# Decoder layer on one core: q and k transposed by DMA in 16-bit halves, probabilities joined by VectorE, other banks for two gates

## The chip, the cores and the metric

The kernel runs on 1 core of one Trainium2 chip. The metric is the device time of one execution in microseconds (us). Engines: TensorE (PE for matmuls, PEld for its weight loads), VectorE (DVE), ScalarE (ACT), GpSimd (POOL) and SyncE (SP, which issues the DMAs). L387 is line 387 of the kernel.

## What is computed

One decoder layer for 256 positions of width 1024, in float32:

```python
proj  = x @ W_in                      -> [q | k | v | B | C | h | gate_attn | gate_conv]
y_att = MoBA block-sparse causal attention(q, k, v) @ W_att   (partial rotary on q, k)
y_cnv = (B * causal_dwconv3(C * h)) @ W_cnv
mix   = (sigmoid(g_att) * y_att + sigmoid(g_cnv) * y_cnv) @ W_o
x     = LayerNorm(alpha * x + mix)
u     = causal_dwconv3(x @ W_up);  f = (silu(u_gate) * u_val) @ W_down
x     = LayerNorm(alpha * x + f)
```

There are 8 heads of 64; the rotary turns the first 16 columns of each head. With 256 positions there is one block, so the attention is a plain causal softmax over it.

## The kernel before

**Two words for one.** Every product is made from a high and a low part. ScalarE rounds a float32 weight unit to the matmul's type (`split_h`, L203, "wh"), VectorE subtracts that from the original (`split_l`, L213, "wl"), and TensorE adds up high x high, high x low and low x high. Activations are split in the same way.

**Units and slots.** The weights come in chunks of 1 MB over SP's DMA queue into three buffers (`issue_dma`, L179). A chunk holds two units of 128x1024. After q, k and v (8 chunks, lines 614 to 670) come 28 units: h, c and b of the first half of the convolution, h, c, b of the second, then 16 gates. C0 is the first of them. `slot(u)` writes the program around unit u: its products on TensorE, then the list "pe" and the list "act" of that slot, then `split_h` up to unit u+5, then the list "first", then `split_l` up to u+4, then the list "dve". Nothing is reordered later: each engine runs its own instructions in the order in which they are written, and waits for what they need. `at(C0 + n, part, f)` puts a step at the end of a list, `at_once` at its head.

**A pair of units** (`two_units`, `cols_pair`): the first unit's wide products (L342) fill its PSUM bank, then the second's, then the narrow products (L349) end both. Two units on, ScalarE copies half of the bank out and VectorE adds the other half (`conv_sum_act` and `conv_sum_dve`, L677 and L681; `gate_sum_act` and `gate_sum_dve`, L729 and L733); then the bank is free. `gate` (L736) is the sigmoid.

**PSUM.** There are two pools of four banks each. Their banks are handed out in turn, and the first product in a bank waits until the last reader of the tile that had it before is done. The pool `acc` holds the banks of q and k, then those of the units. The pool `ps` holds the warm-up, v, the transposes of q and k, the scores, the products with v (`attend`) and the gates 0, 1, 6 and 7.

**The attention**, in steps that stand at fixed slots:

- `evac_rows` (L548): ScalarE copies q and k out of PSUM; `rope` (L376 to L379) turns 16 columns of each head in place, on VectorE, in slots 0 and 1.
- `qk_transpose` (L387, slot 2): TensorE turns 16 blocks of 128x128. `qk_h` (L394) and `qk_l` (through L232), slot 3: ScalarE and VectorE split them from PSUM into `qkT`.
- `scores` (L415): q times k for two head pairs, in slots 4 and 9.
- For each of the four head pairs p: `masks_low` (L422, ScalarE, then GpSimd), `masked` (L432, VectorE), `exps` (L444, ScalarE; the first needs a table load), `normalize` (L454, VectorE).
- The probabilities are transposed by DMA, which turns 16-bit elements: `probs_halves` (L462, VectorE) parts the words into a block of low and a block of high halves, `probs_T` (L466) turns 12 blocks of 128x128 over SP's queue, `probs_words` (L470, ScalarE) joins them again.
- `probs_h` (L473) and `probs_l` (L232) split them, `attend` (L485) multiplies by v, `attend_out` (L494, ScalarE and GpSimd), `attend_sum` (L502, VectorE), `attend_h` (L505) and `attend_l` make the input `aT` of the output product.

**The convolution** (`conv1` to `conv4`, L686 to L707) runs beside it. Behind the 28 units come the output products y (two PSUM banks for each of 8 column blocks), the product with W_o, the first norm, and the feed-forward part.

The lists of slots for the four head pairs, before:

```python
    for p, (m, e, n, tr, w, h, l, av) in enumerate(((5, 6, 8, 9, 12, 12, 13, 14), (7, 8, 11, 13, 15, 16, 16, 18),
                                                    (10, 11, 14, 16, 18, 18, 19, 22), (12, 13, 17, 19, 21, 22, 22, 24))):
```

m is masked, e exps, n normalize and probs_halves, tr probs_T, w probs_words, h and l the split, av attend.

## Time and profile before

| | |
|---|---|
| median of 3 runs | 361.46 us (361.29 to 361.51) |
| the profiled execution | 361.25 us |
| its span in the profile | 359.5 us |
| granted TensorE clock | 0.995 |

How to read it: the page gives the busy time of each engine and its share of the span; PE counts matmuls, whose ends are modelled, so PE can look busy while it only goes from one to the next. A waits line is "engine line <- what ended the wait: us in total, times, longest". The chain is what ended last, in order of time: start, length, engine, tile and line. A group line is "line engine operation out<-in shapes xcount | busy us, mean ns of one | idle before". A windows line is the stretch, its length, and the busy time and count of PE, PEld, DVE, ACT and POOL, then the granted clock, the DMA share and GB/s. A timeline line is start, length, engine, line, operation; merged instructions have a count. All times are from the start of the span.

### The profile page before, as it was taken

Reading aid. Unit: us, or ns where it says so; the run is one execution under the profiler, and the core shown is the slowest. Engines: PE = TensorE matmul, PEld = TensorE weight load, DVE = VectorE, ACT = ScalarE, POOL = GpSimd, SP = SyncE. Lnnn points to the kernel's source line nnn. Section 1 sums busy time; section 2 is a strip of 40 time slices with the busy share of each in tenths; the row PEclk is TensorE's granted clock in tenths of the full one; section 3 lists DMA queues with packets and bytes.
Section 4 is the critical chain, followed back from the end, with each engine's and each line's share of the span. In section 5 each row is a group of like instructions: output and inputs, shape, how many; then the busy total and the mean of one; then the engine's idle time right before and its main releaser. Section 6 shows DMA issues by size and latency. Waiting matters only on the chain.

```text
span 359.5 us, 5201 instructions
## 1 busy us (share of the span) xinstructions
PE 352.1 (98%) x1915; PEld 304.3 (85%) x1915; DVE 302.2 (84%) x522; ACT 238.9 (66%) x415; POOL 22.1 (6%) x49
## 2 busy tenths in 40 slices
PE   9999999999999999999999999999999999999993
PEld 8888889888887888888888888888888888988883
DVE  4687987999888989989769789997869696999875
ACT  4586768699999976652557466766647475677800
POOL 2000001100000112310000000000000000000110
PEclk9999999999999999999999999999999999999998
DMA  8979663753955765679061736538091735663002
GB/s 284 323 263 338 221 240 122 246 168 129 261 170 174 301 228 190 216 297 339 15 233 74 277 129 224 202 148 343 19 338 59 295 127 225 233 232 120 1 33 85
DMA packets 17370, 71.20 MB, mean 198 GB/s; under 512 B 7488, under 2 KB 8000, under 8 KB 10304
## 3 DMA queue, kind: packets, MB, share of 16 engines
q1 hardware_dynamic: 16768, 68.77, 53.2%
q0 software_dynamic: 576, 2.10, 2.0%
q8 instruction: 15, 0.25, 0.3%
q14 instruction: 11, 0.09, 0.1%
HBM read 68.24 MB, written 1.05 MB: 193 GB/s over the span
## 4 chain that ended last, share of the span: by engine, by line
PE 78%; ACT 10%; DVE 7%; issue 3%; POOLq 0%; POOL 0%; DVEq 0%; ACTq 0%
PE pb L342 20%; PE pb L349 11%; PE d L324 5%; PE d L325 5%; PE d L326 4%; PE y L342 4%; PE k L614 3%; PE v L614 3%; ACT wh L203 3%; PE q L614 3%; DVE wl L213 2%; PE y L349 2%; PE o L324 2%; PE o L326 2%; PE o L325 2%
## 5 line engine op out<-in xcount | busy, mean ns | idle before, releaser
L213 DVE TENSOR_TENSOR wl<-raw,wh 128x1024 fp32r<-128x1024 f32 x99 | 121.4, 1230 | 25.3 <-ACT wh L203 25.1
L203 ACT ACTIVATE wh<-raw 128x1024 fp32r<-128x1024 f32 x99 | 103.8, 1055 | 30.5 <-DMA raw<-in_wpack 30.3
L342 PE MATMUL pb<-x1T,wh 128*128 128x512 f32 x320 | 76.2, 390 | 0.0
L342 PEld LDWEIGHTS pb<-x1T,wh 128*128 128x128 f32 x320 | 59.7, 188 | 12.1
L349 PEld LDWEIGHTS pb<-x1T,wl 128*128 128x128 f32 x320 | 41.0, 191 | 1.6
L349 PE MATMUL pb<-x1T,wl 128*128 128x256 f32 x320 | 41.5, 283 | 0.0
L342 PE MATMUL g<-xT,wh 128*128 128x512 f32 x128 | 31.6, 393 | 0.6 <-DVE gs L733 0.6
L236 DVE TENSOR_TENSOR wl<-raw,wh 128x1024 fp32r<-128x1024 f32 (+2 forms) x29 | 27.0, 974 | 5.0 <-ACT wh L235 4.8
L235 ACT ACTIVATE wh<-raw 128x1024 fp32r<-128x1024 f32 (+2 forms) x29 | 23.4, 853 | 9.8 <-DMA raw<-in_wpack 5.8
L324 PE MATMUL d<-wh,f 128*128 128x512 f32 x76 | 29.8, 392 | 0.0
L325 PE MATMUL d<-wl,f 128*128 128x512 f32 x76 | 29.8, 391 | 0.0
L326 PE MATMUL d<-wh,f 128*128 128x512 f32 x76 | 29.6, 389 | 0.0
L342 PEld LDWEIGHTS g<-xT,wh 128*128 128x128 f32 x128 | 23.2, 188 | 5.5 <-PE av L486 0.8
L902 ACT ACTIVATE fb<-pb 128x512 f32<-128x512 f32 x20 | 11.9, 595 | 13.1 <-PE pb L349 13.1
L920 DVE SCALAR_TENSOR_TENSOR fc<-fb,consts,fc 128x254 f32<-128x254 f32 x40 | 19.3, 483 | 1.4
L918 DVE SCALAR_TENSOR_TENSOR fc<-fb,consts,fc 128x255 f32<-128x255 f32 x40 | 19.2, 480 | 0.0
L912 ACT ACTIVATE fc<-fb,consts 128x256 f32<-128x256 f32 x40 | 18.0, 499 | 0.6 <-DVE fb L906 0.6
L349 PEld LDWEIGHTS g<-xT,wl 128*128 128x128 f32 x128 | 16.4, 191 | 0.7
L326 PEld LDWEIGHTS d<-wh,f 128*128 128x128 f32 x76 | 14.3, 188 | 3.1
L349 PE MATMUL g<-xT,wl 128*128 128x256 f32 x128 | 16.6, 282 | 0.0
L324 PEld LDWEIGHTS d<-wh,f 128*128 128x128 f32 x76 | 14.3, 189 | 2.6
L325 PEld LDWEIGHTS d<-wl,f 128*128 128x128 f32 x76 | 14.3, 189 | 2.4
(210 smaller groups left out, 595.4 us busy)
## 6 DMA issues: line engine op xcount, KB each, us to landing
raw<-in_wpack SPq DMA_DIRECT2D x55, 1024.0 KB, 5.0
raw<-in_wpack SPq DMA_DIRECT2D x6, 896.0 KB, 6.1
xr<-in_x SPq DMA_DIRECT2D x1, 1024.0 KB, 7.0
ln<-in_ln_g POOLq DMA_DIRECT2D x2, 512.0 KB, 5.7
ln<-in_ln_b POOLq DMA_DIRECT2D x2, 512.0 KB, 6.3
raw<-in_wpack SPq DMA_DIRECT2D x2, 384.0 KB, 4.2
raw<-in_wpack SPq DMA_DIRECT2D x2, 256.0 KB, 3.1
raw<-in_wpack SPq DMA_DIRECT2D x1, 512.0 KB, 6.0
```

What stands on the lines that cost most here:

```text
L203: nc.scalar.activation(units[u]["h"], raw_of(u), AF.Copy)
L213: nc.vector.tensor_tensor(units[u]["l"], raw_of(u), units[u]["h"].bitcast(F32), op=ALU.subtract)
L235: nc.scalar.activation(h, src, AF.Copy)
L236: (eng or nc.vector).tensor_tensor(l, src, h.bitcast(F32), op=ALU.subtract)
L324: nc.tensor.matmul(o, ah, bh, start=start, stop=False)
L325: nc.tensor.matmul(o, ah, bl, start=False, stop=False)
L326: nc.tensor.matmul(o, al, bh, start=False, stop=stop)
L342: nc.tensor.matmul(bank, un["h"][:, k, n0:n0 + P], b[:, k].rearrange("p a s -> p (a s)"), start=k == 0, stop=False)
L349: nc.tensor.matmul(bank[:, 0:S], un["l"][:, k, n0:n0 + P], b[:, k, 0], start=False, stop=k == nk - 1)
L614: nc.tensor.matmul(banks[m][t], (xl if p == 2 else xh)[:, k, t * P:(t + 1) * P], wl if p == 1 else wh, start=k == 0 and p == 0, stop=k == ...
L918: nc.vector.scalar_tensor_tensor(c[:, 1:S], pb[:, a * S:a * S + S - 1], w_ffn(1, j), c[:, 1:S], op0=ALU.mult, op1=ALU.add)
L920: nc.vector.scalar_tensor_tensor(c[:, 2:S], pb[:, a * S:a * S + S - 2], w_ffn(0, j), c[:, 2:S], op0=ALU.mult, op1=ALU.add)
```

## The change

- q and k are gathered in their own pool of four banks (`QK`, two tiles of two banks). `qk_plain` copies the columns that rope leaves alone, as 16-bit halves, from PSUM to `qkH` on ScalarE; rope reads PSUM and writes its 16 columns there as halves.
- `qk_transpose` is a DMA transpose of 128 x 2048 halves for each half of the positions, on SP's queue, in slot 0. `qk_words` (ScalarE) joins the halves, in slots 4, 4, 5 and 6; `qk_h` and `qk_l` follow in the same slots and read SBUF.
- The pool of q and k is closed in slot 2, and its four banks become the pool `ps`. The warm-up and v take `acc` banks, and the low part of v comes after rope.
- `scores` stand in slots 5 and 10. The slots of the later steps move by up to one or two; `probs_T` stands right behind `probs_halves`.
- `probs_words` is a VectorE copy.
- `conv_sum_act` and `conv_sum_dve` come first in the lists of their slots; the steps of the convolution move by one to three slots.
- The gates in `ps` are 2, 3, 6 and 7 in place of 0, 1, 6 and 7.

```diff
@@ pools
-    ps_pool = single.enter_context(tc.tile_pool(name="ps", bufs=4, space=bass.MemoryType.PSUM))
+    ps_pool = single.enter_context(tc.tile_pool(name="qk", bufs=2, space=bass.MemoryType.PSUM))
...
-    warm = ps_bank("warm")
+    warm = acc_bank("warm")
@@ q and k
-    qk = big.tile([P, 2, 2, AW], F32, tag="rows", name="qk")
-    qkT = big.tile([P, 2, KT, S], F32R, tag="b16", name="qkT")
+    QK = [ps_pool.tile([P, 2, AW], F32, tag="qk", name=f"qk{t}") for t in range(2)]
+    qkH = big.tile([P, 2, 2, 2 * AW], U16, tag="rows", name="qkH")
+    qkHT = big.tile([P, 2, 16, P], U16, tag="x", name="qkHT")
+    qkT = big.tile([P, 2, 2, KT, P], F32R, tag="b16", name="qkT")
+    def qk_plain(t, m):
+
+        src = QK[t][:, m].bitcast(U16).rearrange("p (h d w) -> p w h d", d=HD, w=2)
+        dst = qkH[:, t].rearrange("p w (m h d) -> p w m h d", m=2, d=HD)
+        nc.scalar.activation(dst[:, :, m, :, 16:HD], src[:, :, :, 16:HD], AF.Copy)
+
     def rope(t):
-        xv = qk[:, t].rearrange("p a (h d) -> p (a h) d", d=HD)[:, :, 0:16].rearrange("p h (i f) -> p h i f", i=2)
+        xv = QK[t].rearrange("p a (h d) -> p (a h) d", d=HD)[:, :, 0:16].rearrange("p h (i f) -> p h i f", i=2)
...
-        nc.vector.tensor_tensor(xv[:, :, 0, :], a[:, :, 0, :], b[:, :, 1, :], op=ALU.subtract)
-        nc.vector.tensor_tensor(xv[:, :, 1, :], a[:, :, 1, :], b[:, :, 0, :], op=ALU.add)
-
-    def qk_transpose(g2):
-
-        b = ps_bank(f"qkt{g2}")
-        for gi in range(2):
-            g = 2 * g2 + gi
-            for t in range(2):
-                nc.tensor.transpose(b[:, gi * 256 + t * P:gi * 256 + (t + 1) * P],
-                                    qk[:, t, g // 4, (g % 4) * P:(g % 4 + 1) * P], ident)
-        QB[g2] = b.rearrange("p (g t) -> p g t", g=2)
...
+        nc.vector.tensor_tensor(a[:, :, 0, :], a[:, :, 0, :], b[:, :, 1, :], op=ALU.subtract)
+        nc.vector.tensor_tensor(a[:, :, 1, :], a[:, :, 1, :], b[:, :, 0, :], op=ALU.add)
+        dst = qkH[:, t].rearrange("p w (h d) -> p w h d", d=HD)[:, :, :, 0:16]
+        nc.vector.tensor_copy(dst, a.rearrange("p h i f -> p (h i f)").bitcast(U16).rearrange("p (h d w) -> p w h d", d=16, w=2))
+
+    def qk_transpose(t):
+        nc.sync.dma_start_transpose(qkHT[:, t], qkH[:, t].rearrange("p w n -> p (w n)"))
+
+    def qk_words(e, t):
+
+        w = QW[e, t] = scratch([P, 2, S], f"qw{e}{t}", tag="pr", bufs=2)
+        src = qkHT[:, t].rearrange("p (w m g) q -> p m (g q) w", w=2, m=2)[:, :, e * 256:(e + 1) * 256]
+        nc.scalar.activation(w.rearrange("p m n -> p (m n)").bitcast(U16).rearrange("p (m n w) -> p m n w", m=2, w=2), src, AF.Copy)
...
+    def qk_h(e, t):
+        nc.scalar.activation(qk_part(0, e, t), QW[e, t], AF.Copy)
+
+    def qk_l(e, t):
+        low(qk_part(1, e, t), QW[e, t], qk_part(0, e, t))
@@ probabilities
-        nc.scalar.activation(words(p), halves[:, 1].rearrange("p (h n) -> p h n", h=2), AF.Copy)
+        nc.vector.tensor_copy(words(p), halves[:, 1].rearrange("p (h n) -> p h n", h=2))
@@ v and the pool
+    def evac_v():
         for t in range(2):
...
+            h, _, b = v_parts(t)
+            nc.scalar.activation(h, b, AF.Copy)
+
+    def v_low(t):
+        h, l, b = v_parts(t)
+        low(l, b, h)
+
+    def open_ps():
+        nonlocal ps_pool
+        single.close()
+        ps_pool = single.enter_context(tc.tile_pool(name="ps", bufs=4, space=bass.MemoryType.PSUM))
@@ slots
     for t in range(2):
-        at(C0 + t, "first", rope, t)
-    for g2 in (0, 2, 1, 3):
-        at(C0 + 2, "pe", qk_transpose, g2)
-        at(C0 + 3, "act", qk_h, g2)
-        at(C0 + 3, "dve", qk_l, g2)
-
-    at(C0 + 4, "pe", scores, (0, 1))
-    at(C0 + 9, "pe", scores, (2, 3))
-    for p, (m, e, n, tr, w, h, l, av) in enumerate(((5, 6, 8, 9, 12, 12, 13, 14), (7, 8, 11, 13, 15, 16, 16, 18),
-                                                    (10, 11, 14, 16, 18, 18, 19, 22), (12, 13, 17, 19, 21, 22, 22, 24))):
+        at(C0, "first", rope, t)
+        at(C0, "first", qk_transpose, t)
+    for t in range(2):
+        at(C0, "first", v_low, t)
+    at(C0 + 2, "first", open_ps)
+    for i in range(4):
+        u = C0 + (4, 4, 5, 6)[i]
+        at(u, "act", qk_words, i // 2, i % 2)
+        at(u, "act", qk_h, i // 2, i % 2)
+        at(u, "dve", qk_l, i // 2, i % 2)
+
+    at(C0 + 5, "pe", scores, (0, 1))
+    at(C0 + 10, "pe", scores, (2, 3))
+    for p, (m, e, n, w, h, l, av) in enumerate(((6, 7, 8, 11, 12, 13, 15), (7, 8, 12, 15, 16, 16, 18),
+                                                (11, 12, 15, 18, 19, 19, 21), (13, 14, 18, 21, 22, 22, 24))):
...
-        at(C0 + tr, "pe", probs_T, p)
-        at(C0 + w, "act", probs_words, p)
+        at(C0 + n, "dve", probs_T, p)
+        at(C0 + w, "dve", probs_words, p)
...
-        at(C0 + av + (4 if p == 0 else 3), "act", attend_h, p)
-        at(C0 + av + (4 if p < 2 else 3), "dve", attend_l, p)
+        at(C0 + av + 3 + (p != 3), "act", attend_h, p)
+        at(C0 + av + 3 + (p != 3), "dve", attend_l, p)
@@ q, k, v
-    banks = [[acc_bank(f"{m}{t}") for t in range(2)] for m in "qk"] + [[ps_bank(f"v{t}") for t in range(2)]]
+    banks = [[QK[t][:, m] for t in range(2)] for m in range(2)] + [[acc_bank(f"v{t}") for t in range(2)]]
...
-                    evac_rows(m, banks[m])
+                    for t in range(2):
+                        qk_plain(t, m)
                 else:
-                    evac_v(banks[m])
+                    evac_v()
@@ convolution
-    for pr, (c1, c2, c3, c4) in enumerate(((6, (9, 9), 11, 14), (15, (18, 21), 22, 24))):
+    for pr, (c1, c2, c3, c4) in enumerate(((8, (9, 10), 14, 17), (17, (19, 21), 23, 25))):
...
-                at(U[(off, pr)] + e + 2, "act", conv_sum_act, nm, pr, e)
-                at(U[(off, pr)] + e + 2, "dve", conv_sum_dve, nm, pr, e)
+                at_once(U[(off, pr)] + e + 2, "act", conv_sum_act, nm, pr, e)
+                at_once(U[(off, pr)] + e + 2, "dve", conv_sum_dve, nm, pr, e)
@@ gates
-        GB[j], GB[j + 1] = two_units(U[("g", 0)] + j, [f"g{j + e}" for e in range(2)], ps_bank if j in (0, 6) else acc_bank)
+        GB[j], GB[j + 1] = two_units(U[("g", 0)] + j, [f"g{j + e}" for e in range(2)], ps_bank if j in (2, 6) else acc_bank)
```

The operands of `scores` follow the new layout of `qkT` (position half before column block); its matmuls have the same number and widths.

More of the change, by code (lines that the diff above doesn't have):

```diff
@@ L377, in rope, with qk_part @@
         nc.vector.tensor_tensor(b, xv, si, op=ALU.mult)
[L378 to L397 removed]
+        nc.vector.tensor_tensor(a[:, :, 0, :], a[:, :, 0, :], b[:, :, 1, :], op=ALU.subtract)
[4 more added lines that the diff above has]
+        nc.sync.dma_start_transpose(qkHT[:, t], qkH[:, t].rearrange("p w n -> p (w n)"))
+    QW = {}
+    def qk_words(e, t):
+        w = QW[e, t] = scratch([P, 2, S], f"qw{e}{t}", tag="pr", bufs=2)
+        src = qkHT[:, t].rearrange("p (w m g) q -> p m (g q) w", w=2, m=2)[:, :, e * 256:(e + 1) * 256]
+        nc.scalar.activation(w.rearrange("p m n -> p (m n)").bitcast(U16).rearrange("p (m n w) -> p m n w", m=2, w=2), src, AF.Copy)
+    def qk_part(a, e, t):
+        return qkT[:, a, t].rearrange("p (m g) q -> p m (g q)", m=2)[:, :, e * 256:(e + 1) * 256]
+    def qk_h(e, t):
+        nc.scalar.activation(qk_part(0, e, t), QW[e, t], AF.Copy)
+    def qk_l(e, t):
+        low(qk_part(1, e, t), QW[e, t], qk_part(0, e, t))
     SB, SM, PR = {}, {}, {}
@@ L412, in scores @@
                         o = SB[p][j][:, t * 256:t * 256 + n]
-                        if t == 0 and a == 0:
-                            o = SB[p][j][:, 0:256].rearrange("p (a n) -> p a n", a=2)
-                        nc.tensor.matmul(o, qkT[hs, a, p, t * P:(t + 1) * P], qkT[hs, b, 4 + p, 0:n],
-                                         start=a == 0 and b != 1, stop=a == 1)
+                        k = qkT[hs, b, 0, 4 + p]
+                        if t == 1:
+                            k = qkT[hs, b, :, 4 + p]
+                        if t == 1 or a == 0:
+                            o = SB[p][j][:, t * 256:t * 256 + 256].rearrange("p (a n) -> p a n", a=2)
+                        nc.tensor.matmul(o, qkT[hs, a, t, p], k, start=a == 0 and b != 1, stop=a == 1)
     def masks_low(p):
```

15 lines of the change are left out of this document (3 added, 12 removed).

## Prediction

> **What bounds the kernel now.** I read the head of the page first, then the waits of TensorE, the chain of waits, the busy time by stretches, and last the timeline around the attention work. Unit 0 is the first h unit (C0); "slot n" is the work written beside unit n; wl5, gs3 and so on are named by unit or gate number, and a number after a step of the attention is its head pair.
>
> ```profile
> span 359.5 us, 5201 instructions
> ...
> PE 352.1 (98%) x1915; PEld 304.3 (85%) x1915; DVE 302.2 (84%) x522; ACT 238.9 (66%) x415; POOL 22.1 (6%) x49
> ```
>
> ```profile
> PE warm L249 <- PEq L1172: 0.8, 1, 0.8
> PE g L342 <- DVE gs L733: 0.6, 1, 0.6
> ```
>
> TensorE is busy 98% of the span, and in the middle of the kernel it waits once, for 0.6 us, until VectorE has read a gate's PSUM bank. So only two things can change the time: TensorE work that goes away, and waits that appear or go. Over the whole span VectorE (84%) and ScalarE (66%) seem to have room; in the stage that is changed they have not:
>
> ```profile
> 37.65:125.11 87.46, 86.91 (x526) 76.05 (x525) 78.11 (x161) 75.44 (x150) 6.55 (x8) 1.00 0.61 200
> 62.28:95.00 32.72, 32.72 (x199) 28.66 (x199) 31.00 (x70) 28.99 (x63) 2.51 (x3) 1.00 0.64 193
> 62.28:105.08 42.80, 42.80 (x259) 37.65 (x259) 39.83 (x86) 38.87 (x80) 3.38 (x4) 1.00 0.67 201
> 76.00:124.00 48.00, 47.45 (x272) 41.45 (x271) 42.60 (x78) 47.02 (x86) 3.35 (x4) 1.00 0.67 218
> ```
>
> The columns are the stretch, its length, and the busy time of PE, PEld, DVE, ACT and POOL. From 76 to 124 us ScalarE works 47.02 of 48 us and VectorE 42.60. Over the whole attention stage (37.65 to 125.11) VectorE works 78.11 of 87.46 us. All three engines are nearly full, and TensorE is first by a hair. A microsecond taken from TensorE alone is one that the two others have to give as well.
>
> **The change, part by part.** What leaves TensorE, and the pieces that the later steps need:
>
> ```profile
> 42.83 1.85 PE c L342 x8
> 44.68 1.75 PE qkt L387 x16
> ...
> 48.26 1.91 PE c L349 x16
> ...
> 54.73 0.33 ACT lo L422 x2
> 55.08 1.28 ACT L444
> 56.37 1.00 ACT sm L444 x5
> 57.56 0.68 ACT sm L444 x3
> 58.24 0.27 ACT cb L677
> 58.51 0.96 ACT wh L203
> ```
>
> The 16 transposes of q and k hold TensorE's path for 1.75 us, and they go. With the 0.6 us wait, which can go too, at most 2.35 us are to be had. The score matmuls keep their count and widths, so they cost what they cost.
>
> ScalarE and VectorE, by group in 37 to 124 us (count | busy, mean ns of one | idle before):
>
> ```profile
> L203 ACT ACTIVATE wh<-raw 128x1024 fp32r<-128x1024 f32 x29 | 30.4, 1059 | 0.1
> L470 ACT ACTIVATE sm<-halves 128x1536 uint16<-128x1536 uint16 x4 | 7.8, 1961 | 0.0
> L473 ACT ACTIVATE vpt<-sm 128x768 fp32r<-128x768 f32 x4 | 3.4, 844 | 0.1
> L394 ACT ACTIVATE qkT<-qkt 128x512 fp32r<-128x512 f32 x4 | 2.1, 602 | 1.9 <-PE qkt L387 1.9
> L422 ACT ACTIVATE lo<-s 128x128 f32<-128x128 f32 x8 | 1.8, 285 | 4.8 <-PE s L415 4.8
> ```
>
> ```profile
> L213 DVE TENSOR_TENSOR wl<-raw,wh 128x1024 fp32r<-128x1024 f32 x28 | 34.4, 1232 | 3.5 <-ACT wh L203 3.4
> L462 DVE COPY halves<-sm 128x1536 uint16<-128x1536 uint16 x4 | 3.8, 960 | 0.1
> L502 DVE TENSOR_TENSOR ac<-av,ac 64x256 f32<-64x256 f32 x8 | 3.3, 417 | 0.1
> L232 DVE TENSOR_TENSOR qkT<-qkt,qkT 128x512 fp32r<-128x512 f32 x4 | 2.5, 683 | 0.0
> L454 DVE TENSOR_SCALAR sm<-sm,st 128x256 f32<-128x256 f32 x8 | 2.4, 349 | 0.0
> L686 DVE TENSOR_TENSOR z<-cc,ch 128x512 f32<-128x512 f32 x2 | 1.4, 676 | 0.0
> ```
>
> *probs_words.* Four copies of 1961 ns leave ScalarE (7.8 us) and come to VectorE. No row shows that copy there. The nearest is its mirror, L462: same engine, same 1536 halves, strided on the other side, 960 ns. The far end is what the same copy takes on ScalarE, 1961 ns. I take 0.96, so VectorE gets 4 x 0.96 = 3.84 us. VectorE now also waits for the transposed halves itself, with the mask sums and weight splits queued behind it, and TensorE waits for those.
>
> *qk_words.* Four new ScalarE copies of 1024 halves. Between L203's price for 1024 words (0.96 us a step in the chain) and L470's rate (1961 x 1024 / 1536 = 1.31 us, 1.2 as a step, since neighbours overlap by 0.1) I take 1.2. [...] *qk_plain*: four copies of 768 halves, 0.84 (L473) to 0.98 us (half of L470), in place of two pairs like the one at 34.10 below (1.11 us): at most 1.7 us more, before 41 us. The cover is the 1.9 us that ScalarE idles before qkT (L394's row) and the wait for c0 that now ends it; were the copies twice as dear, wh4 to wh8 would be late by some 4 us, and each is needed over 5 us later.
>
> *rope.* One more copy each, of 512 halves: between L454's 0.35 and half of L462, so 0.4 us. VectorE's sum for the stage is then 78.11 + 3.84 + 2 x 0.4 = 82.8 us. If TensorE gave its 2.35 us, the stage would be 85.1 us long: VectorE could idle 2.3 us in it, where it idles 9.35 now.
>
> *The two q and k transposes.* They sit on SP behind rope. The nearest rows are those of the probabilities (12 blocks each; these have 16):
>
> ```profile
> L466 SPq DMA_TRANSPOSE halves<-halves x4: 1280/1500/2242, 65.6 to 98.1; - x4
> ...
> DMA to landing us min/median/max: 3.7/3.7/7.1
> ```
>
> From the timeline, the work that they stand behind:
>
> ```profile
> 34.10 1.11 ACT L548 ACTIVATE qk<-q 128x512 f32<-128x512 f32 x2
> ...
> 38.86 0.42 DVE L376 TENSOR_TENSOR ra<-qk,cs 128x256 f32<-128x256 f32 x1
> ...
> 40.06 1.22 DVE L213 TENSOR_TENSOR wl<-raw,wh 128x1024 fp32r<-128x1024 f32 x1
> ...
> 51.94 1.43 PE L415 MATMUL s<-qkT 64*128 64x256 f32 x20
> ```
>
> From 34.1 ScalarE does two qk_plain, wh3 and the third: 38.1 us; wl3 ends at 37.1 + 1.1 = 38.2. Rope took 1.2 us (38.86 to 40.06) and gets its copy of 0.4, so its first half ends at about 39.9 and its second at 41.5. With 4/3 of 3.7 us for the landing and 2.0 us of issue each, the halves are there at about 45 and 47 us; even 49 does no harm, because ScalarE comes to qk_words behind c0, whose bank is full at 50.2 - 1.75 - 1.0 = 47.5, and scores (1.4 us, 51.94) are due at 55.3 - 1.4 = 53.9 (step 1). The weight load behind them on SP is that of chunk 13, and its buffer is not free before wl5 at about 45 (41.5, two v_low of 0.6, two splits of 1.13). The probabilities' transposes move one list further on; loads behind them wait for later splits anyway.
>
> *At nothing*: the warm-up and v in the other pool (the c units then wait for v_low, which ends at 42.1 and 42.7, before they start at 42.8 and 44.7); open_ps (closed long before scores); conv sums first in their slot (a few 0.3 us pieces change places). What they cost without cover is the overrun itself.
>
> *Where it ends on the path.* The ends of the sum are these moments of the run before:
>
> ```profile
> 57.03 3.51 PEld L342 LDWEIGHTS h<-xT,wh 128*128 128x128 f32 x16
> ...
> 62.28 1.22 DVE L213 TENSOR_TENSOR wl<-raw,wh 128x1024 fp32r<-128x1024 f32 x1
> ...
> 94.51 0.19 PEld L485 LDWEIGHTS av<-vpt 128*128 128x128 f32 x1
> ...
> 94.65 0.42 DVE L733 TENSOR_TENSOR gs<-g,gs 128x256 f32<-128x256 f32 x1
> ...
> 104.65 1.70 PEld L342 LDWEIGHTS g<-xT,wh 128*128 128x128 f32 x8
> ```
>
> Step 1. TensorE starts unit 6 at 57.03 with the scores of pairs 0 and 1 behind it. Without the transposes that is 55.3, and the scores now end right there, one unit later in the order. From 55.3 ScalarE has, in a row: four lo (4 x 0.28), qk_words 1.2, qk_h 0.5, wh11 0.96, a conv sum 0.27, the table load 1.28, exps 1.87 (56.37 to 58.24), wh12 0.96: together 8.1 us. So VectorE can start wl12, the head of slot 8, at 63.4; before it was 62.28. TensorE at that point is 1.75 us earlier.
>
> Step 2. From wl12 to gs6 VectorE had 39.83 us of work (62.28 to 105.08). It gets three words copies (2.9) and conv1 of the first pair, which comes from slot 6 to slot 8 (0.68): 43.4 us. The 3.0 us that it idled there I take as gone, since it is now later than all that it waited for; that is the low end, and 3.0 the high one. So gs6 ends at 63.4 + 43.4 = 106.8.
>
> Step 3. attend 2 now stands behind unit 21, and its first bank is that of g6 (g2 and g3 took the pool's banks 0 and 1, attend 0 banks 2 and 3, g6 bank 0, attend 1 banks 1 and 2). TensorE starts unit 22 at 104.65 before, so it gets to attend 2 at 102.9 and waits until 106.8: 3.9 us. About 2 us of it fall earlier, at attend 1: there TensorE comes at 94.51 - 1.75 = 92.8, its bank is g3's, and gs3, which ended at 95.07, is at 63.4 + 31.00 + 1.92 + 0.68, less conv1 of the second pair (0.68), attend_sum (2 x 0.42) and conv4 (0.68, as L232), which now stand behind it: 94.8.
>
> After that VectorE has less to do per unit, and the last thing asked of it (aT for the first output product) is ready in time. **Sum:** -1.75 - 0.6 + 3.9 = +1.55 us. The profiled execution took 361.25 us (span 359.5 and 1.75 around it), so 362.8 by it; the median of the runs is 361.46, and on that it is 363.0. About 0.2% (0.7 us) is what a measurement here can tell from no change.
>
> **The rivals.**
>
> *A, VectorE keeps up, faster.* ScalarE is the fuller engine from 76 to 124 us (47.02 of 48), and the change takes 7.8 us from it there; VectorE's idle time is mostly waiting for ScalarE (3.4 us in L213's row alone). If the order of slots lets VectorE run ahead, gs6 is there by 102.9 and all of 2.35 us is gained: 359.1. Against it: it would have to be 3.9 us earlier than step 2 has it, although that has no idle time left. It decides where VectorE's work from wl12 is 39.5 us and not 43.4, or the PSUM banks come in another order. *The Trainium skill, "Perfetto Trace Analysis", "Identifying the Most-Contended Engine", counts occupancy as a fair measure for Scalar and Vector and would have the fuller one relieved first; by that rule this is the outcome.*
>
> *B, the transposes land late, slower still.* If both go behind a weight load (7.1 us x 4/3 = 9.5) and one after the other (4.9 more), the second lands at 54.3; words, qk_h and qk_l (1.2, 0.5, 0.7) put scores at 56.7, 2.8 us late, and every step above shifts: 365.8. For it speaks the 7.1; against it that the load beside them starts after wl3, 1.7 us ahead of the first. *The Trainium skill, "VectorE: DVE Perf Modes", "Rules for kernel authors", would have 128x128 transposes on TensorE if PSUM will do, which speaks against this change; its 1309 ns per block ("The three transpose paths") would make 32 blocks in a row an estimated 42 us, but here 12 blocks landed in 3.7 us.*
>
> *C, the copy on VectorE does not get L462's price.* At 1.96 us, three copies before gs6 put it 3.0 us later: 366.0.
>
> **How the numbers follow.** Forecast 0.52, A 0.30, B 0.10, C 0.08. The forecast's own range is 362.0 (qk_words at L203's price, and half a microsecond less of VectorE work than the rows add up to) to 366.0 (3.0 us idle kept). Of A I give 0.22 to faster and 0.08 to a part of the gain that ends within 0.2%; of the forecast 0.07 lies within. So faster 0.22, same 0.15, slower 0.63. The range that should hold 8 in 10 goes from 359.9, which leaves out the full gain, to 366.0.
>
> **What would show it.** No transposes on TensorE near 44 us, and scores ending near 55.3. A new wait of TensorE for gs (L733's line) or for attend_sum ahead of attend 1 and attend 2, 3 to 5 us in all. VectorE at 97% or more from 62 to 105 us, ScalarE with gaps there. words on VectorE near 0.96 us. gs6 ending near 106.8 and gs3 near 94.5. I am wrong if TensorE shows no such waits (A), or if its wait stands in front of scores (B).

## The result, and the profile after

The changed kernel takes 365.98 us (median of six runs, 364.48 to 366.61), the kernel before 361.49 us on the same chip (six runs, 361.29 to 363.04). The ratio is 1.011, with a 95% interval of 1.008 to 1.014: slower by 4.5 us by the medians. The prediction said 363.0, with a range up to 366.0. The profiled executions of two experiments, e5 and e9, fell into a disturbance of the chip; these two are told by their times alone.

The head of the page of the changed kernel, to be laid beside the one of before:

```profile
span 364.8 us, 5184 instructions
...
PE 352.9 (97%) x1899; PEld 303.7 (83%) x1899; DVE 307.3 (84%) x528; ACT 236.4 (65%) x415; POOL 22.7 (6%) x49
```

TensorE has 16 instructions fewer, the transposes, and is yet 0.8 us longer "busy"; why is seen below. VectorE has 5.1 us more. Next, what TensorE waited for (us in total, times, longest):

```profile
PE av L499 <- DVE gs L761: 2.5, 2, 1.9
PE g L342 <- DVE gs L761: 1.8, 1, 1.8
...
PE qk L657 <- ACT wh L235: 0.8, 1, 0.8
PE qk L641 <- ACT qkH L376: 0.2, 1, 0.2
```

The last two belong to the start of the kernel. One wait of 0.6 us for a gate sum has become three of 4.3 us together. Two of these stand ahead of `attend`, as forecast; one of 1.8 us stands ahead of a gate. The timeline of TensorE says where (start, duration, and in brackets the wait before it):

```profile
94.61 2.11 PE L342 MATMUL g<-xT,wh 128*128 128x512 f32 x8 [1.83 <-DVE gs L761]
97.24 0.47 PE L499 MATMUL av<-vpt 128*128 128x512 f32 x1 [0.51 <-DVE gs L761]
...
101.86 3.82 PE L342 MATMUL g<-xT,wh 128*128 128x512 f32 x16
...
109.52 0.50 PE L499 MATMUL av<-vpt 128*128 128x512 f32 x1 [1.94 <-DVE gs L761]
...
110.36 5.43 PE L342 MATMUL g<-xT,wh 128*128 128x512 f32 x16
```

The first wait is at gate 6, the second at attend 1, the third at attend 2. The last line is the one to stop at: the same 16 products that take 3.82 us at 101.86 take 5.43 us right behind the third wait. The stretches of that time say why (the third number from the end is the granted clock):

```profile
109.00:111.00 2.00, 1.48 (x6) 1.24 (x7) 1.94 (x5) 1.50 (x4) 0.00 (x0) 0.87 0.57 238
111.00:113.00 2.00, 2.00 (x6) 1.51 (x6) 1.97 (x4) 1.62 (x5) 0.00 (x0) 0.50 0.27 45
113.00:115.00 2.00, 2.00 (x9) 1.59 (x8) 1.96 (x4) 1.94 (x6) 0.40 (x1) 0.77 0.93 352
```

From about 110.5 to 113.9 us the clock was granted at half. TensorE counts as busy there, so this loss is in no list of waits: it costs 5.43 - 3.82 = 1.6 us.

Not every execution seems to pay this. Of the six, three had a mean granted clock of 0.992 or 0.993 and took 366.3 to 366.6 us; the other three had 0.997 or 0.998 and took 364.5 to 365.7. A half clock of 3.4 us in a span of 365 lowers the mean by 0.005, which is just this difference, and the two groups lie 1.45 us apart by their means. The profiled execution (0.993) is of the first group. That the second group had no half clock is likely; no trace of it was kept.

VectorE's sums that these waits stand for, from its timeline, are those of gates 2, 3 and 6:

```profile
94.14 0.42 DVE L761 TENSOR_TENSOR gs<-g,gs 128x256 f32<-128x256 f32 x1
...
96.68 0.41 DVE L761 TENSOR_TENSOR gs<-g,gs 128x256 f32<-128x256 f32 x1
...
109.05 0.42 DVE L761 TENSOR_TENSOR gs<-g,gs 128x256 f32<-128x256 f32 x1
```

**One account for all profiles.** The middle of the kernel runs from the first product of unit 0 to the first product of y. In the kernel before, in its timeline:

```profile
37.13 3.79 PE L342 MATMUL h<-xT,wh 128*128 128x512 f32 x16
...
123.94 1.09 PE L342 MATMUL y<-yT,wh 128*128 128x512 f32 x4
```

and in the changed kernel:

```profile
38.67 2.65 PE L342 MATMUL h<-xT,wh 128*128 128x512 f32 x11
...
129.42 1.09 PE L342 MATMUL y<-yT,wh 128*128 128x512 f32 x4
```

So the middle took 86.8 us and takes 90.8. If the waits (0.6 and 4.3) and the half clock (1.6) are taken off, 86.2 and 84.9 are left: the transposes' 1.75 us did go, 1.3 of it by this account, and 5.3 us were given back. The part behind the first y is the same, 235.6 and 235.4 us. The rest is the start, which comes 1.5 us later.

### The profile page after: what moved, and what is told of

It is laid out like the page before. It is cut to its first block, busy times and chain, and to the rows that moved or that the text cites. A ratio compares the mean times of both kernels' runs of the same rounds, so it can differ in the third digit from the quotient of the medians.

```text
span 364.8 us, 5184 instructions
## 1 busy us (share of the span) xinstructions
PE 352.9 (97%) x1899; PEld 303.7 (83%) x1899; DVE 307.3 (84%) x528; ACT 236.4 (65%) x415; POOL 22.7 (6%) x49
## 3 DMA queue, kind: packets, MB, share of 16 engines
HBM read 68.24 MB, written 1.05 MB: 190 GB/s over the span
## 4 chain that ended last, share of the span: by engine, by line
PE 77%; DVE 11%; ACT 5%; issue 4%; DMA 1%; POOLq 0%; DVEq 0%; POOL 0%; SPq 0%
PE pb L342 20%; PE pb L349 10%; PE qk L641 6%; PE d L324 4%; PE d L325 4%; PE d L326 4%; DVE wl L213 4%; PE y L342 4%; PE g L342 3%; PE v L641 3%; PE y L349 2%; PE o L324 2%; PE o L326 2%; PE o L325 2%; PE g L349 2%
## 5 line engine op out<-in xcount | busy, mean ns | idle before, releaser
L213 DVE TENSOR_TENSOR wl<-raw,wh 128x1024 fp32r<-128x1024 f32 x99 | 121.5, 1232 | 22.8 <-ACT wh L203 22.3
L342 PE MATMUL g<-xT,wh 128*128 128x512 f32 x128 | 32.7, 408 | 1.8 <-DVE gs L761 1.8
L342 PEld LDWEIGHTS g<-xT,wh 128*128 128x128 f32 x128 | 24.5, 197 | 7.3 <-DVE gs L761 2.0
L641 PE MATMUL qk<-wh,xT 128*128 128x512 f32 x60 | 19.3, 391 | 0.2 <-ACT qkH L376 0.2
```

What stands on the lines that cost most here:

```text
L213: nc.vector.tensor_tensor(units[u]["l"], raw_of(u), units[u]["h"].bitcast(F32), op=ALU.subtract)
L342: nc.tensor.matmul(bank, un["h"][:, k, n0:n0 + P], b[:, k].rearrange("p a s -> p (a s)"), start=k == 0, stop=False)
L641: nc.tensor.matmul(banks[m][t], (xl if p == 2 else xh)[:, k, t * P:(t + 1) * P], wl if p == 1 else wh, start=k == 0 and p == 0, stop=k == ...
```

## The experiments

Twelve kernels, each timed beside the kernel before on the same chip. The medians of before were 361.8 us (beside e1 to e4), 361.4 (e5 to e8), 361.1 (e9 to e11) and 361.5 (e12). The names of the theories are those of the expectations: L, VectorE's load ahead of the gate sums makes the waits; S, ScalarE is the engine to relieve; D, the q and k transposes by DMA are late; T, the pool's order of banks makes the waits whatever VectorE does.

**e1. The words back on ScalarE.**

```diff
-        nc.vector.tensor_copy(words(p), halves[:, 1].rearrange("p (h n) -> p h n", h=2))
+        nc.scalar.activation(words(p), halves[:, 1].rearrange("p (h n) -> p h n", h=2), AF.Copy)
...
-        at(C0 + w, "dve", probs_words, p)
+        at(C0 + w, "act", probs_words, p)
```

> The changed kernel with one part undone: probs_words on ScalarE again, in the same slots. Theory L (VectorE runs behind, and TensorE waits for PSUM banks that VectorE has not read yet; in the changed kernel 4.3 us in all, and the 1.9 us wait ahead of attend 2 is followed by 3.4 us at half the granted clock, worth 1.7 us): VectorE loses 2.9 us of copies ahead of gs6, so TensorE's waits fall to about 1.4 us, the half clock goes, and the time is 361 to 362. Rival S (ScalarE is the fuller engine, and the copies were rightly taken from it): ScalarE gets 1.96 us a copy back, the waits stay at 4 us or grow, now behind ScalarE, and the time is 365 or more. Rival D (the new DMA transposes of q and k delay the stage): nothing changes, 364.5 to 366.5.

365.42 us, ratio 1.010 (1.009 to 1.012): no better than the changed kernel. L's number missed. S's number was met, but not its waits of 4 us or more: they are 3.2 us in all. The busy time of one stretch shows both engines full, and a half clock in it (0.86 in the mean), behind a wait of 2.4 us at attend 1:

```profile
95.00:107.00 12.00, 9.63 (x45) 7.97 (x44) 11.80 (x22) 11.94 (x22) 1.16 (x1) 0.86 0.47 128
```

VectorE 11.80 and ScalarE 11.94 of 12 us: work that is taken from the one finds no room on the other here. L as "VectorE alone" is already too simple.

**e2. The words left out.**

```diff
-        at(C0 + w, "dve", probs_words, p)
```

> The changed kernel with probs_words left out on every engine: the probabilities go on without having been transposed, everything else runs. Theory L: 2.9 us less VectorE work ahead of gs6, so waits of 1.4 us in place of 4.3, no half clock: 360.5 to 361.5, and about the time of the run with the copies on ScalarE or a little less. Rival D: as the changed kernel, 364.5 to 366.5. Theory T (the pool's order of banks holds TensorE up, whatever VectorE has to do): waits at g6, attend 1 and attend 2 stay within 0.5 us of 4.3.

362.2 us (361.55 to 363.69), ratio 1.0018 (1.0007 to 1.0029). The 4.4 us of copies are worth 3.4 us of time (the ratios differ by 0.0093), and TensorE's timeline keeps two waits of 2.0 us in all, both short of 1.3, with no half clock:

```profile
95.58 0.47 PE L499 MATMUL av<-vpt 128*128 128x512 f32 x1 [1.25 <-DVE gs L760]
...
106.59 0.50 PE L499 MATMUL av<-vpt 128*128 128x512 f32 x1 [0.70 <-DVE gs L760]
```

T and D are refuted: same order of banks, same DMAs, and the waits more than halve. L has the sign and most of the size (it said 360.5 to 361.5). The 2.0 us of waits that stay without any copy are made by the other parts of the change, and without this whole step it is still no faster than before.

**e3. The words on VectorE, alone in the kernel before.**

```diff
-        nc.scalar.activation(words(p), halves[:, 1].rearrange("p (h n) -> p h n", h=2), AF.Copy)
+        nc.vector.tensor_copy(words(p), halves[:, 1].rearrange("p (h n) -> p h n", h=2))
...
-        at(C0 + w, "act", probs_words, p)
+        at(C0 + w, "dve", probs_words, p)
```

The slots of words for pair 0 are 11 (12), and of h for pair 2, 19 (18).

> The kernel before with this one part of the change alone: probs_words on VectorE (words of the first pair one slot earlier, probs_h of the third one slot later, so that the order holds). q and k stay with TensorE. Theory L: VectorE's work in the stage goes from 78.1 to 82.0 us of 87.5 and its lag grows by up to 2.9 us at gs6, less what it no longer waits for ScalarE; the bank waits stay under 2 us: 361.3 to 363. Rival S: ScalarE was the bound, 7.8 us go from it, and the one wait of 0.6 us goes: 360.8 to 361.0.

361.89 us, ratio 1.0007 (0.9998 to 1.0015): no change. S is refuted here; ScalarE got its room (25.84 of 33 us where it had 29.20) and nothing came of it. But the copies cost nothing either, though VectorE is as full as in the changed kernel:

```profile
62.00:95.00 33.00, 33.00 (x203) 28.95 (x203) 32.07 (x75) 25.84 (x61) 2.52 (x3) 1.00 0.62 188
95.00:107.00 12.00, 12.00 (x71) 10.58 (x70) 11.83 (x21) 8.73 (x18) 1.59 (x1) 1.00 0.72 175
```

A full VectorE does not by itself stop TensorE. What differs is how soon a bank is wanted back. In the kernel before, gate 6 takes the bank of gate 0; VectorE's row of that sum, from its timeline:

```profile
83.60 0.42 DVE L733 TENSOR_TENSOR gs<-g,gs 128x256 f32<-128x256 f32 x1
```

TensorE starts gate 6 at 92.89, so there are 8.9 us between. In the changed kernel gate 6 takes the bank of gate 2, whose sum ends at 94.56, when TensorE has stood there since 92.78. So the order of banks has its part: it took the reserve away on which the extra work could have been drawn. That is read from the two traces. TensorE also comes 1.75 us sooner without the transposes, and ScalarE has a new row ahead of slot 8 (e6 below); both take from the same reserve, and how the three share it was not tried. The order of before was not tried in the changed kernel: gate 0 would need the bank that masked 2 leaves at about 85.4 there, and TensorE is at gate 0 at 75.2.

**e4. No DMA transposes of q and k.**

```diff
-        src = qkHT[:, t].rearrange("p (w m g) q -> p m (g q) w", w=2, m=2)[:, :, e * 256:(e + 1) * 256]
+        src = qkH[:, t].rearrange("p w (m n) -> p m n w", m=2)[:, :, e * 256:(e + 1) * 256]
...
-        at(C0, "first", qk_transpose, t)
```

> The changed kernel with the two DMA transposes of q and k left out: qk_words reads the halves as they were written, in the same shapes, so q and k are not transposed; every other instruction stays. Theory L: ScalarE waits for c0 and not for the transposes, so nothing moves: 364.5 to 366.5, waits of 4.3 us as before. Rival D: the transposes or the traffic beside them cost the time; without them the waits fall by over 1 us and the time by as much.

364.93 us, ratio 1.010 (1.008 to 1.012). D is refuted, and so is the prediction's rival B: the same waits on gate banks without them. One line differs (this execution took 367.6 us, the five others 364.5 to 365.3):

```profile
PE av L499 <- DVE gs L760: 2.5, 2, 1.9
PE g L342 <- DVE gs L760: 1.8, 1, 1.8
PE qk L640 <- ACT qkH L376: 1.7, 1, 1.7
```

The wait of the last line is in the changed kernel too, with 0.2 us, and is the subject of the next run.

**e5. qk_plain behind k's products.** q and k of one block of rows now share a tile of two PSUM banks. k's last products write the second bank while qk_plain still reads the first, and TensorE waits for that.

```diff
-                if m < 2:
-                    for t in range(2):
-                        qk_plain(t, m)
-                else:
+                if m == 1:
+                    for mm in range(2):
+                        for t in range(2):
+                            qk_plain(t, mm)
+                elif m == 2:
```

> The four qk_plain copies are issued together behind the last products of k, and no longer two behind those of q and two behind those of k; all else is as in the changed kernel. Theory M (the two-bank tile costs time): k's products no longer wait for a copy of q's bank in the same tile, TensorE's row of waits loses its 0.2 us on qk_plain, the first unit begins some 0.5 us earlier against the first product, and the time is 365.3 to 365.7. Rival N: ScalarE now does all four copies ahead of the evacuation of v and of the first unit's halves, so TensorE waits there instead, and the time is 366 or over. Theory L (VectorE behind by the bank waits of 4.3 us) says that these waits stay within 0.5 us of that in either case.

365.31 us, ratio 1.010 (1.008 to 1.012): 0.7 us less than the changed kernel by the medians and 0.4 by the ratios, as M has it, but the intervals overlap, and by time alone it stays open. The traces of the others carry the point: with the order of the changed kernel the wait is 0.2 us in six profiles and 1.2 (e6) and 1.7 (e4) in two, and with the order of e5 it is gone in both that were read (e11 and e12). It is part of the late start.

**e6. qk_words left out.**

```diff
-        w = QW[e, t] = scratch([P, 2, S], f"qw{e}{t}", tag="pr", bufs=2)
-        src = qkHT[:, t].rearrange("p (w m g) q -> p m (g q) w", w=2, m=2)[:, :, e * 256:(e + 1) * 256]
-        nc.scalar.activation(w.rearrange("p m n -> p (m n)").bitcast(U16).rearrange("p (m n w) -> p m n w", m=2, w=2), src, AF.Copy)
+        QW[e, t] = xh[:, 2 * t:2 * t + 2, :].bitcast(F32)
```

> The four qk_words copies are left out, and qk_h and qk_l read finite words of x of the same shape instead (the output is then not the reference's); the DMA transposes stay. This takes 4 x 1.08 us off ScalarE, two of them ahead of the work that the head of slot 8 waits for. Theory R (the prediction's first step: ScalarE's row between the end of the scores and slot 8 sets when VectorE's full stretch begins): that stretch begins 1.2 us earlier or more, the waits on gate banks fall from 4.3 to 2 to 3 us, the half clock mostly goes, and the time is 362.5 to 364.2. Rival F: VectorE's start is set by the scores and not by ScalarE, the waits stay at 4 us or over, and the time stays within 0.7 us of 366.

364.68 us, ratio 1.008 (1.007 to 1.010): 1.3 us less by the medians and 1.0 by the ratios, whose intervals overlap; it is just above R's range. TensorE's timeline says more:

```profile
93.30 2.11 PE L342 MATMUL g<-xT,wh 128*128 128x512 f32 x8 [0.35 <-DVE gs L759]
95.94 0.47 PE L497 MATMUL av<-vpt 128*128 128x512 f32 x1 [0.53 <-DVE gs L759]
108.22 0.50 PE L497 MATMUL av<-vpt 128*128 128x512 f32 x1 [1.95 <-DVE gs L759]
```

The wait at gate 6 falls by 1.48 us: ScalarE's row ahead of slot 8 does set when VectorE's full stretch starts (R), here 25.1 us behind unit 0 in place of 26.2. The waits are 2.8 us in all, as R said. But the wait at attend 2 stays (1.95 against 1.94), with the half clock behind it. So the lag is formed in two stretches, and an earlier start takes only from the first. The second is a race of its own: from the sum of gate 3 to that of gate 6 VectorE takes 109.05 - 96.68 = 12.37 us in the changed kernel and 107.75 - 95.38 = 12.37 here, where it took 104.66 - 94.65 = 10.0 in the kernel before. TensorE's work between the two, from attend 1 (97.24) to attend 2 (109.52 less the 1.94 of waiting), is 10.3 us. The difference is the wait, within 0.1 us.

**e7. The words on GpSimd.**

```diff
-        nc.vector.tensor_copy(words(p), halves[:, 1].rearrange("p (h n) -> p h n", h=2))
+        nc.gpsimd.tensor_copy(words(p), halves[:, 1].rearrange("p (h n) -> p h n", h=2))
```

> The joining of the halves goes to GpSimd, which is 6% busy, in the same slots. From its rows in the changed kernel (128x256 words added in 0.79 to 0.96 us) 1536 halves are an estimated 3 to 6 us each there. Theory L (VectorE's load makes the waits): VectorE loses 4.4 us as in the run without the copies, the waits on gate banks fall to 1.5 to 2.5 us, and the time is 362.0 to 363.5, as near to the 362.2 of that run as the later words allow. Rival G: the words come so late, or VectorE's own instructions become so much longer beside GpSimd's, that probs_h or attend waits for them, and the time is 365 or over.

366.21 us, ratio 1.014 (1.013 to 1.016): no gain, and the waits are 4.0 us. G is right, by its second half. The groups of VectorE between 74 and 108 us, here:

```profile
L730 DVE TENSOR_TENSOR ct<-cb,ct 128x512 f32<-128x512 f32 x1 | 2.0, 2046 | 0.0
L232 DVE TENSOR_TENSOR yT<-ct,yT 128x512 fp32r<-128x512 f32 x1 | 1.9, 1912 | 0.0
```

and in the changed kernel:

```profile
L232 DVE TENSOR_TENSOR yT<-ct,yT 128x512 fp32r<-128x512 f32 x1 | 0.7, 694 | 0.0
L730 DVE TENSOR_TENSOR ct<-cb,ct 128x512 f32<-128x512 f32 x1 | 0.7, 682 | 0.0
```

Two instructions that met a GpSimd copy (1.95 to 2.87 us each) became 1.36 and 1.22 us longer. Two splits of weights that met the other two copies (L213, at 73.49 and 109.83 us in the timeline) took 2.90 and 1.66 us, where such a split takes 1.24 in the changed kernel. Together the four are some 4.7 us longer, as much as the 4.4 us of copies that VectorE was spared. This is what the Trainium skill has in "SBUF — State Buffer", "SBUF: two separate sides": VectorE with two SBUF inputs and GpSimd reading SBUF share a pair of ports, and one of them waits out the other's whole instruction. The trace agrees: all four have two inputs in SBUF, and a gate sum with one input in PSUM, at 86.33 us beside the same copy as L730, took its usual 0.42 us.

**e8. attend 1 and 2 one slot later.**

```diff
-    for p, (m, e, n, w, h, l, av) in enumerate(((6, 7, 8, 11, 12, 13, 15), (7, 8, 12, 15, 16, 16, 18),
-                                                (11, 12, 15, 18, 19, 19, 21), (13, 14, 18, 21, 22, 22, 24))):
+    for p, (m, e, n, w, h, l, av) in enumerate(((6, 7, 8, 11, 12, 13, 15), (7, 8, 12, 15, 16, 16, 19),
+                                                (11, 12, 15, 18, 19, 19, 22), (13, 14, 18, 21, 22, 22, 24))):
```

> attend of pairs 1 and 2 is issued one slot later (19 and 22), and with it what follows on it; VectorE's work is the same. By the order of the banks attend 1 then takes two that attend 0 left, and attend 2 those of gates 6 and 7, a slot after the last of them is summed. Theory T2 (the waits are there because attend follows too closely on the sums of the gate banks, and nothing else needs VectorE so soon): the waits at attend go, that at gate 6 (1.8 us) stays, no half clock follows, and the time is 362.2 to 363.5. Rival V (VectorE is behind whatever waits for it): the waits come back at gate 7, at attend 2 or at the start of y, 3.5 us or more in all, and the time is 365 to 366.5.

364.37 us, ratio 1.009 (1.007 to 1.010), between the two theories. TensorE's timeline:

```profile
93.82 2.12 PE L342 MATMUL g<-xT,wh 128*128 128x512 f32 x8 [1.67 <-DVE gs L761]
96.45 2.09 PE L342 MATMUL g<-xT,wh 128*128 128x512 f32 x8 [0.51 <-DVE gs L761]
109.95 0.47 PE L499 MATMUL av<-vpt 128*128 128x512 f32 x1 [1.05 <-DVE gs L761]
```

The 0.5 us of attend 1 moves to gate 7, the 1.94 of attend 2 becomes 1.05, and 3.2 us are left in all (V's mechanism). The longest is now 1.67 us and no half clock follows it, which is worth 1.6 us more by the account above. So the size of a single wait matters beside the sum. But this execution is the shortest of the six, at a mean clock of 0.999; four of the others had 0.995 or 0.996 and took 363.9 to 365.3 us, so they may not all have been spared.

**e9, e10, e11. VectorE's work pushed out of the stretch; the words shared.** e9 puts later what y alone needs (the first part of the diff); e10 gives the words of pairs 0 and 1 to ScalarE (the second part); e11 does both, with the edit of e5.

```diff
-    for pr, (c1, c2, c3, c4) in enumerate(((8, (9, 10), 14, 17), (17, (19, 21), 23, 25))):
+    for pr, (c1, c2, c3, c4) in enumerate(((8, (9, 10), 18, 21), (21, (22, 23), 25, 27))):
...
-        at(C0 + av + 3 + (p != 3), "act", attend_h, p)
-        at(C0 + av + 3 + (p != 3), "dve", attend_l, p)
+        at(C0 + av + (7, 4, 4, 3)[p], "act", attend_h, p)
+        at(C0 + av + (7, 4, 4, 3)[p], "dve", attend_l, p)
...
-        nc.vector.tensor_copy(words(p), halves[:, 1].rearrange("p (h n) -> p h n", h=2))
+        src = halves[:, 1].rearrange("p (h n) -> p h n", h=2)
+        if p < 2:
+            nc.scalar.activation(words(p), src, AF.Copy)
+        else:
+            nc.vector.tensor_copy(words(p), src)
...
-        at(C0 + w, "dve", probs_words, p)
+        at(C0 + w, "act" if p < 2 else "dve", probs_words, p)
```

> Work of VectorE that nothing needs before y is issued later, and nothing else is changed: conv3 and conv4 of pair 0 in slots 18 and 21 (14 and 17), conv1, conv2, conv3, conv4 of pair 1 in 21, 22 and 23, 25, 27 (17, 19 and 21, 23, 25), attend_l of pair 0 in 22 (19). By the changed kernel's rows this takes 0.68 us of VectorE past the sum of gate 2 that gate 6 waits for, and 0.69 + 0.68 + 0.99 + 0.41 = 2.8 us past the sum of gate 6 that attend 2 waits for. Theory L (VectorE's load ahead of each of these sums makes the waits): gate 6's wait falls from 1.8 to about 1.1, attend 2's from 1.9 to near none, no half clock follows, and the time is 361.8 to 363. Rival V2 (the stretch has no slack, the moved work only meets another end): VectorE is late at y or at a later gate, TensorE waits there, and the time is 365 or over. Rival C2 (the waits come from the order of the banks or from ScalarE's half of the sum): waits and time stay.

> probs_words of pairs 0 and 1 on ScalarE (slots 11 and 15, where it is 26 us busy of 33), of pairs 2 and 3 on VectorE as in the changed kernel. VectorE loses 1.25 + 1.04 = 2.3 us ahead of the sum of gate 2, ScalarE gains 2 x 1.96 us. Theory L: gate 6's wait of 1.8 us goes, attend 2's of 1.9 us stays (nothing is moved between the sums of gates 3 and 6), with the half clock behind it, and the time is 363.5 to 364.5. Rival S2 (ScalarE is as full as VectorE there too): VectorE waits for ScalarE, gate 6's wait stays over 1.3 us, and the time is 365.3 or over, as with all four on ScalarE.

> The two edits above together (conv and attend_l later, words shared) and the four qk_plain copies behind k's products. Theory L: with 3 us less ahead of gate 2's sum and 5.1 us less ahead of gate 6's than in the changed kernel, all three waits go but a few tenths, no half clock follows, and with 0.4 us less at the start the time is 360.2 to 361.5, which is the kernel before (361.4) or just under it. Rival V2: 363 or over, with a wait at y, at a later gate or at the first unit in place of those that went.

e9: 369.95 us, ratio 1.023 (1.021 to 1.025); e10: 365.11, 1.011 (1.009 to 1.012); e11: 368.22, 1.019 (1.018 to 1.021). All three of L's numbers missed; V2's 365 or over in e9 and 363 or over in e11 were met. TensorE's timeline in e11:

```profile
92.59 2.11 PE L342 MATMUL g<-xT,wh 128*128 128x512 f32 x8 [0.57 <-DVE gs L766]
97.07 0.47 PE L503 MATMUL av<-vpt 128*128 128x512 f32 x1 [2.37 <-DVE gs L766]
118.63 2.08 PE L342 MATMUL g<-xT,wh 128*128 128x512 f32 x8 [0.88 <-DVE gs L766]
130.58 0.73 PE L342 MATMUL y<-yT,wh 128*128 128x512 f32 x2 [1.85 <-DVE yT L232]
```

The wait at attend 2 is gone, for two reasons. VectorE takes 107.71 - 96.51 = 11.2 us from the sum of gate 3 to that of gate 6 in place of 12.37, and the half clock, now behind attend 1, makes TensorE's work in that race 1.6 us longer. The second does more: in e10, where no work left this race and the half clock stands in the same place, little of the wait remains in TensorE's timeline:

```profile
109.63 0.50 PE L503 MATMUL av<-vpt 128*128 128x512 f32 x1 [0.42 <-DVE gs L765]
```

The work that left the race in e11 is late elsewhere: at a later gate (0.88) and at y itself (1.85), which rival V2 had said. That the same makes e9 slow is likely; why e9 is 1.7 us above e11 is open. In e10 and e11 the wait at gate 6 falls to 0.6 us, as L said, but at attend 1 stands a new 2.37, although VectorE has 2.3 us less to do there. VectorE's timeline in e10 says why:

```profile
92.41 0.42 DVE L765 TENSOR_TENSOR gs<-g,gs 128x256 f32<-128x256 f32 x1 [0.68 <-ACT gs L761]
94.72 0.96 DVE L232 TENSOR_TENSOR vpt<-sm,vpt 128x768 fp32r<-128x768 f32 x1 [1.89 <-ACT vpt L491]
95.66 1.23 DVE L213 TENSOR_TENSOR wl<-raw,wh 128x1024 fp32r<-128x1024 f32 x1
96.80 0.42 DVE L765 TENSOR_TENSOR gs<-g,gs 128x256 f32<-128x256 f32 x1
```

VectorE stands still for 1.89 us at probs_l of pair 1, until ScalarE has its high part, and the sum of gate 3 is queued behind. ScalarE's timeline there:

```profile
87.04 1.95 ACT L486 ACTIVATE sm<-halves 128x1536 uint16<-128x1536 uint16 x1
...
89.90 1.28 ACT L768 ACT_TABLE_LOAD   x1
...
93.83 0.85 ACT L491 ACTIVATE vpt<-sm 128x768 fp32r<-128x768 f32 x1
```

It works without a gap from 84.06 to 99.37: exps, the weights, the words, the table load, the gates, four pieces of attend_out (1.5 us), and only then the high part. Here ScalarE is late, and VectorE passes it on.

**e12. probs_h of pair 1 ahead of attend_out of pair 0**, with the edits of e10, e5 and e8.

```diff
-        at(C0 + h, "act", probs_h, p)
+        (at_once if p == 1 else at)(C0 + h, "act", probs_h, p)
```

> Words shared (pairs 0 and 1 on ScalarE), attend of pairs 1 and 2 in slots 19 and 22, the four qk_plain copies behind k's products, and new: probs_h of pair 1 is issued ahead of attend_out of pair 0 on ScalarE. Theory K (after the run with the shared words: VectorE's queue is held 1.9 us at probs_l of pair 1, which waits for ScalarE's probs_h of pair 1 behind 1.5 us of attend_out, and the sum of gate 3 stands behind it, so neither engine's load alone makes the waits but the way in which the two take turns): VectorE's idle time ahead of that probs_l falls to 0.4 us or less, the sum of gate 3 comes 1.5 us earlier against gate 6, the waits on gate banks are 1.2 us or less in all, there is no half clock, and the time is 361.2 to 362.8. Theory L (VectorE's load alone): the waits are gone for its 2.3 us less, with or without the order of probs_h, and the time is the same 361 to 362.5, but VectorE's idle time stays 1.9 us. Rival V3 (attend_out, now later, holds the sums behind it): the wait comes back at gate 7 or attend 1, 2 us or more, and the time is 364 or over.

363.27 us, ratio 1.0054 (1.0040 to 1.0067): the best version with all its parts, and still slower than before. VectorE's timeline:

```profile
91.97 0.96 DVE L232 TENSOR_TENSOR vpt<-sm,vpt 128x768 fp32r<-128x768 f32 x1 [0.31 <-ACT vpt L491]
94.49 1.23 DVE L213 TENSOR_TENSOR wl<-raw,wh 128x1024 fp32r<-128x1024 f32 x1 [1.56 <-ACT wh L203]
95.63 0.41 DVE L766 TENSOR_TENSOR gs<-g,gs 128x256 f32<-128x256 f32 x1
```

The idle time at probs_l fell from 1.89 to 0.31 us, as K said, and came back one instruction on: 1.56 us for the next high part of the weights, which now stands behind attend_out. The sum of gate 3 is no earlier against gate 6, and TensorE waits 2.38 us for it, at gate 7 (V3's mechanism; the time is between the two). Turning ScalarE's row round only moved the wait; from 84 to 98.2 us the row has no gap.

**The account over all profiles.** "Middle" is from the first product of unit 0 to the first of y; "rest" is the middle less the waits in it and less 1.6 us where a half clock was seen, all in the profiled executions.

| kernel | middle, us | waits | half clock | rest |
|---|---|---|---|---|
| before | 86.8 | 0.6 | no | 86.2 |
| e3, words alone | 87.4 | 1.1 | no | 86.3 |
| changed | 90.8 | 4.3 | yes | 84.9 |
| e1, words on ScalarE | 89.7 | 3.2 | yes | 84.9 |
| e2, words left out | 86.5 | 2.0 | no | 84.6 |
| e4, no DMA transposes | 90.7 | 4.3 | yes | 84.8 |
| e6, no qk_words | 89.3 | 2.8 | yes | 84.8 |
| e7, words on GpSimd | 91.0 | 4.2 | yes | 85.2 |
| e8, attends later | 88.1 | 3.2 | no | 84.9 |
| e10, words shared | 89.8 | 3.4 | yes | 84.9 |
| e11, three edits | 90.1 | 3.8 | yes | 84.7 |
| e12, row in order | 88.8 | 2.7 | yes | 84.4 |

The rest is 86.2 and 86.3 with the transposes on TensorE and 84.4 to 85.2 without. The gain was there in each; within the 0.8 us by which the rests differ, the waits and the clock are all that was added in the middle.

## Why the prediction was right, and where its sizes were off

**What leaves TensorE: right.** 1.75 us were forecast; 1.0 to 1.9 us is the difference of the rests.

**Step 1, the start of VectorE's stretch: right.** Less the 1.55 us by which unit 0 starts later, scores end at 55.3 and wl12 starts at 63.3; 55.3 and 63.4 were forecast. e6 shows that the row on ScalarE is the cause: without qk_words the first wait falls by 1.5 us. qk_words took 1.18 us by its group (1.2 forecast), the rope copy 0.43 (0.4):

```profile
L400 ACT ACTIVATE qw<-qkHT 128x1024 uint16<-128x1024 uint16 x4 | 4.7, 1182 | 0.0
```

**Step 2, VectorE's 43.4 us without idle time: right, and 1.1 us short.** The sum of gate 6 ended 1.1 us later than forecast (109.47, less 1.55, against 106.8); 0.8 us of idle time stayed, and the words took more than their mirror:

```profile
L484 DVE COPY sm<-halves 128x1536 uint16<-128x1536 uint16 x4 | 4.4, 1093 | 0.0
```

The prediction took VectorE's lag as one sum from wl12 to the sum of gate 6, and for the total this held: in e6 an earlier start took 1.45 us from all waits together. What the sum does not show is where the lag is formed. A better start takes from the part up to the sums of gates 2 and 3, and leaves the part from there to the sum of gate 6.

**Step 3, the waits: 3.9 us forecast, 4.3 measured**, on gate banks, at about the time said: about 2 us up to attend 1 and the rest at attend 2 were forecast, 2.3 and 1.9 came. That 1.8 of it would stand at gate 6 itself was not seen, though the text said that gate 6 takes gate 2's bank.

**The sum, +1.55 forecast, +4.5 measured.** The terms on which it rests were about right, and two were missing. The waits were taken at their length, and one of 1.9 us costs 1.6 us more through the clock. And the start was taken as unchanged: 1.5 us, of which the two-bank tile of q and k explains 0.2 in the profile of the changed kernel (1.2 and 1.7 in two others). The other visible part is a first piece of weights that landed later in that execution (its first copy began at 5.55, at 4.38 before): TensorE waited 0.75 us for it (L657). But six profiles of the changed order in which that copy began at 4.3 to 4.9 start unit 0 at 37.99 to 39.57, so how much of the late start belongs to the change is open. That 365.98 still lies inside the stated range, by 0.02 us, is luck: its upper end was reached by 3.0 us of idle time of VectorE, of which 0.8 stayed, and neither the clock nor the start was in it.

**Rival A, VectorE keeps up:** refuted by the trace, and its premise by e3, where 7.8 us less on ScalarE changed nothing. The rule that was weighed there, from the Trainium skill, "Perfetto Trace Analysis", "Identifying the Most-Contended Engine", is to work first on the engine that is busiest by occupancy; to relieve ScalarE by it gave 361.89 against 361.76 us here. **Rival B, the transposes are late:** refuted by e4. **Rival C, a dearer copy:** an eighth of the way, 1.09 us where 0.96 and 1.96 were the ends.

**What the runs leave as the cause.** The words on VectorE cost 3.4 us in the changed kernel (e2) and 0.3 us, no more than can be measured, in the kernel before (e3). ScalarE (e1, e10, e12) and GpSimd (e7) did not take them without a loss: in this stretch VectorE and ScalarE take turns, each waits for the other's half of the work, and extra work on either is passed on to the sum that TensorE waits for. With the words in place, ScalarE's new row is worth 1.5 us of waiting (e6); how much of the 2.0 us that stay without them is its share was not tried. That the banks of gates 2 and 3 are wanted back at once, where that of gate 0 had 8.9 us, is the likely reason for the difference between e2 and e3; it is read from the traces and was not tried by itself.

## What to carry to other kernels

Where two helper engines take turns, ask for each buffer that they release how long it lies free before it is wanted again; in these runs the same extra work cost nothing that could be measured where the reserve was 8.9 us, and 3.4 of its 4.4 us where there was none, on whichever of the two it was put. Moving such work later helps only as far as its own due time allows, as e11's convolution met y. Price a wait of TensorE by its length and by what the clock does behind it.

## What the runs showed of the hardware

A single wait of TensorE of about 1.9 us was enough for the clock to go to half. In the middle of the kernel and at y, over all these profiles, every wait from 1.90 us on was followed by it (1.90, 1.94, 1.95 twice, and 2.37 or 2.38 four times), and none up to 1.85 us was. These are the twelve profiled executions; the mean clocks of the others suggest that not every execution of the changed kernel had it, so where the border lies is not shown. In e5 and e6 the times part in the same way: 364.2 to 364.9 and 363.0 to 363.5 us at a mean clock of 0.996 to 0.998, 365.7 to 365.8 and 364.6 to 365.3 at 0.992 to 0.994; in e1 they do not. The half clock lasted about 3.4 us and cost 1.6 us. The Trainium skill, "TensorE: Matmul & The Clock Gate", "What's actually happening", has 3.4 us as the window by which the clock is granted, free-running; the length agrees. It asks for an idle window of that length before the clock falls, and here 1.90 us did it; the measurement decides.

A tile of two PSUM banks was one thing to wait for in this program: products into its second bank waited for a ScalarE copy that read only the first, 0.2 to 1.7 us. Whether the banks or the program's own semaphores ask for that was not tried. And a copy of 1536 halves took 1.09 us on VectorE, 1.95 on ScalarE and 1.95 to 2.87 on GpSimd, whose spans in the profile are rough.
